# A mixer and mixture-of-experts layer on one core: 128-row score operands, another row order of the expert weights, fewer overflow branches, and the final norm in a branch of its own

## Chip, core and metric

The kernel runs as one program on 1 core of one Trainium2 chip. The metric is the device time of one execution in microseconds (us). Before the change three runs took 717.22, 716.81 and 714.42 us, median 716.81.

## What is computed

One layer over 256 tokens of 1024 channels, with 256 context tokens beside them, in float32. Cut to what matters here:

```
m = silu(c) @ w_mod + b_mod                       # six vectors: sh1 sc1 g1 sh2 sc2 g2
h = rms_norm(x) * (1 + sc1) + sh1                 # the same for the context tokens
gq, gk, gv, nq, nk, nv, fu, cu, gl = split(h @ w_in)
y_gqa = attention(8 query heads, 2 key/value heads, 256 + 256 keys)   # "g"
y_na  = neighbourhood attention, 8 heads                              # "n"
y_fn, y_cv = 2-D Fourier mixing, convolution of 31 taps
x = x + g1 * (sum of sigmoid(gate) * (branch @ w_branch)) @ w_out
h2 = rms_norm(x) * (1 + sc2) + sh2
# router: the best of 4 groups of experts, in it the best 2 of 4 experts
x = x + g2 * sum_e gate[:, e] * ((silu(a_e) * b_e) @ w_down[e]),  a_e, b_e = split(h2 @ w_gu[e])
out = rms_norm(x)                                 # the final norm
```

There are 16 experts; w_gu[e] is 1024x1024 and w_down[e] 512x1024, so each expert brings 6 MiB of weights, 96 MiB in all.

## The kernel before

**Up to the router.** SyncE (SP) streams weight tiles of 1 MiB. `product` (L290) multiplies them on TensorE in three passes, with a high and a low part of both operands made by ScalarE (L277) and VectorE (L278). Instructions are put in order ahead of time by a planner that sets the projection's matmuls between the steps of the attention, and on VectorE the taps of the convolution (L458) and the sums of the modulation (L194).

**Attention "g" (L482 to L505).** For 8 heads and 2 tiles of 128 queries each, so for 16 score tiles, the scores are two matmuls into one PSUM tile of 128x512. The first multiplies `qG`, which holds the high part of 64 channels in one half of its 128 rows and the low part in the other, by `kT`, the high part of the keys, stacked twice. The second adds high part by low part: it takes the 64 rows of `qG` with the high part and the 64 rows of `kTl`, the low part of the keys, of that group. Then come VectorE's maximum (L487), an exponential on ScalarE (L492), a reciprocal and a product on VectorE (L493, L494), four transposes (L497) and the product with the values (L505). `kTl` is written by one subtraction of 128x128 for each of four key tiles (`split`, L375), `kT` by copies of 64x128 (L385, L386).

**Experts.** They go in 8 pairs. `load_unit` (L630) brings 256 rows of a weight matrix as one tile [128 partitions, 2, 1024]; row k * 128 + p of the unit goes to partition p, so a partition gets two pieces of 4 KB. Up to 64 tokens of an expert are handled in fixed places, in two blocks of 32; the flags of the router say which pairs need the second block (`both`), which experts have more than 64 tokens (`fmore`, up to 128, summed by pair in `fpair`), and which more than 128 (`frest`). A pair's order of work is: the gather of the tokens for a group of 2 pairs (`group_step`, one-hot matmuls "gag" with 128 channels of `xh` and `xl` as the stationary operand), up products of block 1, `If(both)` block 2, `If` overflow up (`more_up`), scatter of the previous pair (adds on `xs`, L905), transposes of the hidden values (L815), **`If` overflow gather of the next pair** (`more_gather`), down products, `If(both)`, `If` overflow down (`more_down`). Each overflow `If` first asks for the pair (L1126) and within it for each expert (L1128). With the inputs here experts 5 and 13, in pairs 2 and 6, are the only ones with an overflow, and no expert has more than 128 tokens.

**End.** After the last scatter each engine with work in it meets `If(frest > 0)` (L1212), a long body that never runs here, and jumps over it. Then the final norm follows: four squares with sums on ScalarE (L1222), three short POOL instructions for each of two token tiles (L1225, L112, L113), four products on VectorE (L1229) and four output DMAs (L1230), two issued by ScalarE and two by SP.

Of the kernel before, what the change touches and what calls it, by code (L numbers as in the profile page):

```python
# [19 lines left out]
P = 128  # L20
D = 1024
# [29 lines left out]
PKW = _off  # L51


@with_exitstack
def mixer_moe(ctx: ExitStack, tc: tile.TileContext, A, out, dbg=None):
# [143 lines left out]
    def mod_cols(i, dst):  # L199

        res = []
        yield from mod_sums(i, res)
        t = pt("md", f"mt_{i}")
        for b in range(NK):
            PE.matmul(t[:, 2 * b : 2 * b + 2], res[0][:, P * b : P * (b + 1)], ones[:, 0:2], start=True, stop=True)
        V.tensor_tensor(dst, t[:, : 2 * NK].rearrange("p (b r) -> p b r", r=2)[:, :, 0],
                        pks("bm")[:, NK * i : NK * (i + 1)], op=ALU.add)
# [320 lines left out]
    def half(h, i):  # L528
# [5 lines left out]
              lambda h, t, i: qG[half(h // 4, i), h // 4, h % 4, 128 * t : 128 * t + 128],  # L534
              lambda h, i: (kTl[half(h // 4, 1)] if i else kT[:, h // 4]).rearrange("p k n -> p (k n)"),
# [156 lines left out]
    for c in range(4):  # L692
        accs = [mm_t(f"wo{c}{t}") for t in range(NT)]
        product(A["w_out"][:, 256 * c : 256 * c + 256], NK,
                [(accs[t][:, :256], tok_major((mh, ml), t)) for t in range(NT)], f"out{c}")
        cs = slice(256 * c, 256 * c + 256)
        for t in range(NT):
            xc = xs[:, t, cs]
            tmp = gp.tile([P, 512], F32, name=f"xo{c}{t}", tag="gt")
            V.tensor_tensor(tmp[:, :256], accs[t][:, :256], g1row[:, cs], op=ALU.mult)  # L700
            V.tensor_tensor(xc, xc, tmp[:, :256], op=ALU.add)
            tp = tr_t(f"x2tr{c}{t}")
            for k in range(2):
                PE.transpose(tp[:, 128 * k : 128 * (k + 1)], xs[:, t, P * (2 * c + k) : P * (2 * c + k + 1)], ident)
# [86 lines left out]
    def low_rows(k0, k1):  # L791
        s = slice(P * k0, P * k1)
# [7 lines left out]
    with tc.issue_after(last_route.ins if hasattr(last_route, "ins") else last_route):  # L800
        low_rows(0, 1)
# [49 lines left out]
    def gather_step(hg, oh, k, name):  # L851
# [108 lines left out]
    def more_gather(e):  # L960
# [20 lines left out]
        for k in range(NK):  # L981
            d = tp[:, CAP * k : CAP * (k + 1)]
            tr(d, rows[:CAP, k // 4, P * (k % 4) : P * (k % 4 + 1)], ident[:CAP, :CAP])
# [39 lines left out]
    def rest(e):  # L1023
# [26 lines left out]
        for f in range(4):  # L1050
            tr(tp[:, 128 * f : 128 * f + 128], si[:, 128 * f : 128 * f + 128], ident)
# [31 lines left out]
    def first_gather(k):  # L1083
        if k:
            with tc.issue_after(after_oh.ins if hasattr(after_oh, "ins") else after_oh):
                low_rows(k, k + 1)
# [37 lines left out]
    def more_of(pair, f):  # L1124

        with tc.If((fpair & (1 << (8 + pair))) > 0):  # L1126
            for e in (2 * pair, 2 * pair + 1):
                with tc.If((fmore & (1 << e)) > 0):  # L1128
                    f(e)
# [24 lines left out]
    for pair in range(NPAIR):  # L1154
# [9 lines left out]
        if pair == NPAIR - 2:  # L1164
            frest = nc.values_load(flags[0:1, 2:3], engines=engs + [ET.SP], min_val=0, max_val=top)
# [26 lines left out]
        if pair + 1 < NPAIR:  # L1192
            more_of(pair + 1, lambda e: rows_of.__setitem__(e, more_gather(e)))
# [10 lines left out]
        more_of(pair, lambda e: more_down(e, rows_of[e][1], si_of[e]))  # L1204
# [6 lines left out]

    with tc.If(frest > 0, label="rest"):  # L1212
# [3 lines left out]


    junk = ep.tile([P, 2, 512], F32, name="junk", tag="ys", bufs=1)
    fss = small.tile([P, NT, 2], F32, name="fss", tag="fss", bufs=1)
    for t in range(NT):  # L1220
        for h in range(2):
            SC.activation(junk[:, h, :], xs[:, t, 512 * h : 512 * h + 512], AF.Square,  # L1222
                          accum_out=fss[:, t, h : h + 1])
        fr = small.tile([P, 2], F32, name=f"fr{t}", tag="rs")
        G.tensor_tensor(fr[:, 0:1], fss[:, t, 0:1], fss[:, t, 1:2], op=ALU.add)  # L1225
        rstd_of(fr[:, 0:1], fr[:, 0:1], D, 1)
        for h in range(2):
            s = slice(512 * h, 512 * h + 512)
            V.scalar_tensor_tensor(xs[:, t, s], xs[:, t, s], fr[:, 0:1], fng[:, s], op0=ALU.mult, op1=ALU.mult)  # L1229
            (nc.sync if h else nc.scalar).dma_start(out[128 * t : 128 * t + 128, s], xs[:, t, s])  # L1230
# [33 lines left out]

def layout(i):
# [8 lines left out]
        n1g=_cols(f["norm1_g"][0]), n2g=_cols(f["norm2_g"][0]),  # L1274
# [5 lines left out]
        wr=f["w_router"].reshape(NK, P, NE).transpose(1, 0, 2).reshape(P, -1), rb8=rows(np.tile(f["router_bias"], NT)),  # L1280
        low4=rows(np.tile(np.tril(np.ones((4, 4)), -1).reshape(-1), 8)), mhalf=np.full((P, 2), -0.5),
        bm=_cols(f["b_mod"][0]),
# [41 lines left out]
```

## Time and profile before

| | |
|---|---|
| runs | 717.22, 716.81, 714.42 us |
| profiled execution, its own time | 722.76 us |
| span of the instructions in it | 721.0 us |
| TensorE busy | 640.1 us, 89% |
| VectorE, ScalarE, POOL busy | 412.8, 265.7, 71.9 us |

PE is TensorE's matmuls and PEld its weight loads, DVE is VectorE, ACT ScalarE, POOL GpSimd and SP SyncE; a "q" behind a name is that engine's sequencer, which handles branches. "Idle" in a row is the time in which the engine did nothing just before, and behind the arrow stands what ended it. The profiled execution is 5.95 us longer than the median of the runs.

### The profile page before, as it was taken

To read this page: it belongs to the slowest core of one execution; us is meant where nothing else is said; L and a number is where in the kernel's file an instruction comes from. 1 tells how busy PE (TensorE), PEld (TensorE's weight loads), DVE (VectorE), ACT (ScalarE), POOL (GpSimd) and SP (SyncE) were. 2 spreads that over 40 slices of the span, in tenths; PEclk is the share of its full clock that TensorE was granted. 3 is DMA by queue.
4 is the path that set the end of the run, shared out by engine and by line. 5 is a ranking of instruction groups with operands and counts; after the bars stand their busy time and mean duration, and the time that the engine had idled before them with its cause. 6 is when DMAs were issued, how large, how long until landed. Compare 5 with 4: busy or idle time off the path is not lost. (4 is left out here: it accounts for less than half of the span.)

```text
span 721.0 us, 12019 instructions
## 1 busy us (share of the span) xinstructions
PE 640.1 (89%) x4721; PEld 443.8 (62%) x4725; DVE 412.8 (57%) x806; ACT 265.7 (37%) x486; POOL 71.9 (10%) x112
## 2 busy tenths in 40 slices
PE   3769899999999998999999967889889979998992
PEld 0269899987887898989899952343324224333230
DVE  0179889988888787585766553351343243303334
ACT  2066947367755533343445441230012111300112
POOL 0123300021302000313111010000000000000001
PEclk9969999999999999999999988899989999999895
DMA  9794582533543696768698560999997999998001
GB/s 362 277 340 130 177 286 64 170 119 118 170 136 99 247 314 210 252 224 264 219 370 287 175 234 4 397 408 407 408 409 285 409 406 409 407 385 347 1 2 62
DMA packets 75121, 180.07 MB, mean 250 GB/s; under 512 B 3104, under 2 KB 39072, under 8 KB 74016
## 3 DMA queue, kind: packets, MB, share of 16 engines
q1 hardware_dynamic: 73232, 173.42, 66.0%
q0 software_dynamic: 1104, 3.15, 1.4%
q10 hardware_dynamic: 704, 2.42, 0.8%
q8 instruction: 52, 0.85, 0.5%
q14 instruction: 29, 0.24, 0.1%
HBM read 177.92 MB, written 1.05 MB: 248 GB/s over the span
## 5 line engine op out<-in xcount | busy, mean ns | idle before, releaser
L812 PE MATMUL gu<-we,hg 128*32 128x512 f32 x832 | 101.5, 606 | 3.7 <-PEq L1126 2.4
L290 PE MATMUL gl<-hhil,wl_gl 128*128 128x256 f32 x256 | 72.9, 287 | 1.8 <-DVE wl_gl L278 1.7
L290 PE MATMUL gl<-hhil,wh_gl 128*128 128x256 f32 x256 | 73.3, 287 | 0.0
L290 PE MATMUL gl<-hlol,wh_gl 128*128 128x256 f32 x256 | 72.3, 283 | 0.0
L812 PEld LDWEIGHTS gu<-we,hg 128*32 128x32 f32 x832 | 28.3, 111 | 68.5 <-issue 59.3
L812 PE MATMUL y<-we,hT 128*32 128x512 f32 x416 | 59.8, 649 | 6.1 <-PEq L1126 5.6
L277 ACT CAST wh_gl<-w_gl 128x1024 fp32r<-128x1024 f32 x32 | 33.1, 1049 | 50.0 <-PE gl L290 25.4
L458 DVE SCALAR_TENSOR_TENSOR cv<-zp,pk,cv 128x256 f32<-128x256 f32 x120 | 51.2, 478 | 0.2
L290 PEld LDWEIGHTS gl<-hhil,wl_gl 128*128 128x128 f32 x256 | 48.0, 188 | 3.9 <-DVE wl_gl L278 3.3
L290 PEld LDWEIGHTS gl<-hhil,wh_gl 128*128 128x128 f32 x256 | 48.1, 188 | 1.5 <-issue 1.5
L290 PEld LDWEIGHTS gl<-hlol,wh_gl 128*128 128x128 f32 x256 | 48.3, 189 | 0.5 <-issue 0.5
L290 PE MATMUL z<-y,wh_br 128*128 128x256 f32 x256 | 47.6, 283 | 0.0
L278 DVE TENSOR_TENSOR wl_gl<-w_gl,wh_gl 128x1024 fp32r<-128x1024 f32 x32 | 41.0, 1294 | 9.8 <-ACT wh_gl L277 9.6
L194 DVE SCALAR_TENSOR_TENSOR acc<-wv,csil,acc 128x512 f32<-128x512 f32 x56 | 40.3, 747 | 7.8 <-DMA wv<-in_w_mod_dram 7.8
L812 PEld LDWEIGHTS y<-we,hT 128*32 128x32 f32 x416 | 14.9, 115 | 42.2 <-issue 39.9
L290 PEld LDWEIGHTS z<-y,wh_br 128*128 128x128 f32 x256 | 39.6, 188 | 0.9 <-issue 0.7
L374 ACT CAST yh<-ys 64x512 fp32r<-64x512 f32 x32 | 19.7, 617 | 51.5 <-DVE ys L894 51.1
L290 PE MATMUL z<-y,wl_br 128*128 128x256 f32 x128 | 36.8, 289 | 1.5 <-DVE wl_br L278 1.5
L894 DVE SCALAR_TENSOR_TENSOR ys<-y,gsl,G 128x512 f32<-128x512 f32 x16 | 12.0, 750 | 37.5 <-PE y L812 17.3
L674 POOL TENSOR_TENSOR merged<-merged,gt 128x512 f32<-128x512 f32 x12 | 19.3, 1610 | 117.6 <-DVE gt L673 117.6
L876 DVE TENSOR_TENSOR si<-si,gu 128x256 f32<-128x256 f32 x16 | 6.6, 418 | 42.5 <-ACT si L875 42.5
L166 PE MATMUL mod<-wm,csil 128*32 128x512 f32 x64 | 15.2, 843 | 14.4 <-DVE csil L155 9.0
(411 smaller groups left out, 1514.0 us busy)
## 6 DMA issues: line engine op xcount, KB each, us to landing
we<-in_w_gu_dram SPq DMA_DIRECT2D x64, 1024.0 KB, 13.3
we<-in_w_down_dram SPq DMA_DIRECT2D x32, 1024.0 KB, 18.4
wv<-in_w_mod_dram SPq DMA_DIRECT2D x16, 1024.0 KB, 5.5
w_gl<-in_w_in_dram SPq DMA_DIRECT2D x16, 1024.0 KB, 5.7
wm<-in_w_mod_dram SPq DMA_DIRECT2D x8, 1024.0 KB, 9.4
w_br<-in_w_branch_dram SPq DMA_DIRECT2D x8, 1024.0 KB, 5.9
w_out<-in_w_out_dram SPq DMA_DIRECT2D x4, 1024.0 KB, 6.4
w_gq<-in_w_in_dram SPq DMA_DIRECT2D x2, 1024.0 KB, 8.1
```

What stands on the lines that cost most here:

```text
L166: PE.matmul(acc[32 * j : 32 * j + 32, :], csil[:, k, :], wm[:, 512 * j : 512 * (j + 1)], start=(k == 0), stop=(k == NK - 1))
L194: V.scalar_tensor_tensor(acc[:, s], wm[:, k % 2, s], csil[:, k, 0:1], acc[:, s], op0=ALU.mult, op1=ALU.add)
L277: SC.copy(w[0], raw[:, s])
L278: sub(w[1], raw[:, s], w[0].bitcast(F32), op=ALU.subtract)
L290: PE.matmul(dst, a, b, start=(k == 0 and wi + xi == 0), stop=(k == kt - 1 and wi == 1))
L374: SC.copy(hi, src)
L458: V.scalar_tensor_tensor(cv[:, ct, :], zp[:, ct, j : j + S], convw[:, ct, j : j + 1], cv[:, ct, :], op0=ALU.mult, op1=ALU.add)
L674: G.tensor_tensor(mt, mt, gts[c], op=ALU.add)
L812: tc.keep_in_program_order(PE.matmul(*a, **k))
L876: V.tensor_tensor(si, si, acc[:, n:], op=ALU.mult)
L894: V.scalar_tensor_tensor(ys, y, gsl, G2[flip], op0=ALU.mult, op1=ALU.mult)
```

## The change

Four things are changed. (1) `kTl` becomes as wide as `kT`: for each group 128 rows, zero in the half that the group doesn't use. The second score matmul then contracts over 128 rows. (2) A weight unit puts rows 2p and 2p + 1 into partition p, one piece of 8 KB. The channels that meet those rows are taken with stride 2 (`chan`) in everything that makes the other operand: gathers, transposes, the low part `xl`, and the packed constants. (3) The overflow gather of the next pair moves behind the down products and shares one outer `If` with the overflow down; the first pair's gather and up share one as well. (4) The final norm becomes a function. It stands in `If(fnone < 1)`, which TensorE doesn't take part in, straight behind the last scatter and ahead of the `rest` body; a second copy stands at the end of that body.

```diff
+def chan(k):
+    return slice(2 * P * (k // 2) + k % 2, 2 * P * (k // 2 + 1), 2)
...
-    kTl = kG[:, 1024:1536].rearrange("p (k n) -> p k n", k=4)
+    kTl = kG[:, 1024:2048].rearrange("p (g k n) -> p g k n", g=2, k=4)
+    for g in range(2):
+        hs = slice(64 - 64 * g, 128 - 64 * g)
+        SC.activation(kTl[hs, g], ident[hs].unsqueeze(1).to_broadcast([64, 4, P]), AF.Copy, scale=0.0)
...
-            split(kh, kTl[:, kt, :], tp[:, :P])
+            SC.copy(kh, tp[:, :P])
+            for g in range(2):
+                hs = slice(64 * g, 64 * g + 64)
+                V.tensor_sub(kTl[hs, g, kt], tp[hs, :P], kh[hs].bitcast(F32))
...
-              lambda h, t, i: qG[half(h // 4, i), h // 4, h % 4, 128 * t : 128 * t + 128],
-              lambda h, i: (kTl[half(h // 4, 1)] if i else kT[:, h // 4]).rearrange("p k n -> p (k n)"),
+              lambda h, t, i: qG[:, h // 4, h % 4, 128 * t : 128 * t + 128],
+              lambda h, i: (kTl if i else kT)[:, h // 4].rearrange("p k n -> p (k n)"),
...
-        nc.sync.dma_start(t, src.rearrange("(k p) n -> p k n", p=P))
+        nc.sync.dma_start(t, src.rearrange("(p k) n -> p k n", k=2))
...
-                mm(g, src[:, t, P * k : P * (k + 1)], oh[t], start=(i == 0), stop=(i == 2 * NT - 1))
+                mm(g, src[:, t, chan(k)], oh[t], start=(i == 0), stop=(i == 2 * NT - 1))
...
-            tr(tp[:, 128 * c : 128 * c + 128], si[:, 128 * c : 128 * c + 128], ident)
+            tr(tp[:, 128 * c : 128 * c + 128], si[:, c::2], ident)
...
+    def more_first():
+        with tc.If((fpair & (1 << 8)) > 0):
+            for e in of(0):
+                if_more(e, lambda e: (rows_for(e), up_for(e)))
...
+    def more_rest(pair):
+        two = pair + 1 < NPAIR
+        with tc.If((fpair & ((3 if two else 1) << (8 + pair))) > 0):
+            for e in of(pair):
+                if_more(e, lambda e: more_down(e, rows_of[e][1], si_of[e]))
+            if two:
+                for e in of(pair + 1):
+                    if_more(e, rows_for)
...
-            frest = nc.values_load(flags[0:1, 2:3], engines=engs + [ET.SP], min_val=0, max_val=top)
+            others = [ET.DVE, ET.Activation, ET.Pool, ET.SP]
+            frest = nc.values_load(flags[0:1, 2:3], engines=[ET.PE] + others, min_val=0, max_val=top)
+            fnone = nc.values_load(flags[0:1, 2:3], engines=others, min_val=0, max_val=top)
...
-        if pair == 0:
-            more_of(0, lambda e: rows_of.__setitem__(e, more_gather(e)))
-        more_of(pair, lambda e: si_of.__setitem__(e, more_up(e, rows_of[e][0])))
+        more_ups(pair) if pair else more_first()
...
-        if pair + 1 < NPAIR:
-            more_of(pair + 1, lambda e: rows_of.__setitem__(e, more_gather(e)))
...
-        more_of(pair, lambda e: more_down(e, rows_of[e][1], si_of[e]))
+        more_rest(pair)
...
+    def final_norm():
+        junk = ep.tile([P, 2, 512], F32, name="junk", tag="ys", bufs=1)
+        for t in range(NT):
+            ...
+    with tc.If(fnone < 1):
+        final_norm()
     with tc.If(frest > 0, label="rest"):
         for e in range(NE):
             with tc.If((frest & (1 << e)) > 0):
                 rest(e)
+        final_norm()
```

The transposes of the normalised rows (L704), the low part `xl` (L794, 16 instructions of 128x128 in both kernels) and the modulation's column matmuls (L205) take `chan` in the same way.

## Rows read from the trace of the kernel before

**Rows 1.** Stretches: length, then busy us by engine, granted clock, DMA share, GB/s.
```profile
60.00:90.00 30.00, 26.77 (x218) 25.69 (x216) 26.82 (x69) 25.16 (x62) 12.22 (x14) 1.00 0.49 149
148.00:185.00 37.00, 37.00 (x270) 27.75 (x270) 31.12 (x66) 26.60 (x54) 7.18 (x14) 1.00 0.31 99
260.00:275.00 15.00, 13.32 (x110) 13.02 (x109) 13.16 (x19) 6.20 (x8) 0.00 (x0) 1.00 0.71 239
450.00:690.00 240.00, 216.83 (x1508) 82.44 (x1512) 81.33 (x163) 39.98 (x77) 3.71 (x14) 0.95 0.89 352
```
**Rows 2.** Timeline of weight loads: start, us, engine, line, operands, shapes, idle before.
```profile
148.49 0.18 PEld L482 LDWEIGHTS sg<-kG,qG 64*128 64x128 f32 x1 [0.24 <-issue]
148.92 0.19 PEld L482 LDWEIGHTS sg<-kG,qG 128*128 128x128 f32 x1 [0.24 <-issue]
```
**Rows 3.** Waits of 148 to 185 us: total us, times, longest.
```profile
PEld sg L482 <- issue: 4.9, 21, 0.3
```
**Rows 4.** Timeline of TensorE, two scatter matmuls of 128 rows in a row.
```profile
468.35 0.39 PE L812 MATMUL sce<-yl,oTe 128*128 128x512 f32 x1
468.58 0.40 PE L812 MATMUL sce<-yh,oTe 128*128 128x512 f32 x1
```
**Rows 5.** Instructions of L385 and L375: ns min/median/max, first and last start.
```profile
L385 ACT CAST kG<-kh x8: 283/296/307, 81.8 to 92.2; 64x128 fp32r<-64x128 f32 x8
L385 ACT CAST qG<-qh x4: 610/616/621, 72.6 to 78.5; 64x512 fp32r<-64x512 f32 x4
...
L375 DVE TENSOR_TENSOR kG<-ktr,kh x4: 283/284/288, 81.6 to 91.8; 128x128 fp32r<-128x128 f32 x4
```
**Rows 6.** Timeline of TensorE, two steps of a gather.
```profile
472.37 0.28 PE L812 MATMUL gag<-ohg,xl 128*128 128x256 f32 x1
472.49 0.28 PE L812 MATMUL gag<-ohg,xh 128*128 128x256 f32 x1
```
**Rows 7.** Instructions of gather loads, and of L360 (stride 2) and L363 (contiguous).
```profile
L812 PEld LDWEIGHTS gag<-ohg,xh x64: 186/188/330, 429.9 to 613.1; 128*128 128x128 f32 x64
...
L360 DVE TENSOR_TENSOR ropet_q<-qq,rsq x4: 284/289/295, 56.0 to 73.9; 128x128 f32<-128x128 f32 x4
...
L363 DVE TENSOR_TENSOR kn<-kk,ropet_k x2: 286/286/287, 79.2 to 82.7; 128x128 f32<-128x128 f32 x2
```
**Rows 8.** Stretches with 8 KB pieces (first) and 4 KB pieces (second).
```profile
16.00:20.60 4.60, 2.00 (x3) 0.27 (x3) 1.24 (x2) 1.85 (x4) 2.58 (x6) 1.00 1.02 424
...
480.00:540.00 60.00, 54.33 (x360) 18.41 (x365) 19.48 (x37) 8.97 (x18) 0.53 (x2) 0.94 1.03 408
```
**Rows 9.** Idle time ahead of instructions that use expert weights: us, times.
```profile
  DMA we<-in_w_gu_dram: 1.9, 4
```
**Rows 10.** TensorE's waits of 440 to 721 us: total us, times, longest.
```profile
PE y L812 <- PEq L1126: 6.0, 9, 2.8
PE gs L812 <- PEq L1126: 3.3, 1, 3.3
...
PE gu L812 <- PEq L1126: 2.4, 5, 0.9
PE gav L812 <- DVE ohv L840: 1.7, 2, 0.9
```
**Rows 11.** ScalarE's sequencer at L1212: ns min/median/max, start us.
```profile
L1212 ACTq COMPARE_BRANCH  x1: 64/64/64, 703.1 to 703.1; - x1
L1212 ACTq EVENT_SEMAPHORE  x1: 17/17/17, 705.7 to 705.7; - x1
```
**Rows 12.** Timeline of all engines at the end.
```profile
708.68 0.69 DVE L905 TENSOR_TENSOR xs<-xs,sce 128x512 f32<-128x512 f32 x1 [0.17 <-PE sce L812]
711.67 0.63 ACT L1222 ACTIVATE junk<-xs 128x512 f32<-128x512 f32 x1 [7.34 <-DVEq L1212]
...
715.67 2.48 SPq L1230 DMA_DIRECT2D out_dram<-xs  x2
...
716.36 1.41 DVE L1229 SCALAR_TENSOR_TENSOR xs<-xs,fr,pk 128x512 f32<-128x512 f32 x2 [0.72 <-POOL fr L113]
```

More of the change, by code (lines that the diff above doesn't have):

```diff
@@ L204, in mod_cols @@
         for b in range(NK):
-            PE.matmul(t[:, 2 * b : 2 * b + 2], res[0][:, P * b : P * (b + 1)], ones[:, 0:2], start=True, stop=True)
+            PE.matmul(t[:, 2 * b : 2 * b + 2], res[0][:, chan(b)], ones[:, 0:2], start=True, stop=True)
         V.tensor_tensor(dst, t[:, : 2 * NK].rearrange("p (b r) -> p b r", r=2)[:, :, 0],
@@ L703, in mixer_moe @@
             for k in range(2):
-                PE.transpose(tp[:, 128 * k : 128 * (k + 1)], xs[:, t, P * (2 * c + k) : P * (2 * c + k + 1)], ident)
+                PE.transpose(tp[:, 128 * k : 128 * (k + 1)], xs[:, t, chan(2 * c + k)], ident)
             SC.copy(tmp[:, 256:], tp[:, :256])
@@ L790, in mixer_moe, with low_rows @@
             last_xh = SC.activation(xh[:, t, :], xs[:, t, :], AF.Copy, scale=rstd[:, t : t + 1])
-    def low_rows(k0, k1):
-        s = slice(P * k0, P * k1)
+    def low_rows(k):
+        s = chan(k)
         for t in range(NT):
@@ L800, in mixer_moe @@
     with tc.issue_after(last_route.ins if hasattr(last_route, "ins") else last_route):
-        low_rows(0, 1)
+        low_rows(0)
     dump("key", key)
@@ L982, in more_gather @@
             d = tp[:, CAP * k : CAP * (k + 1)]
-            tr(d, rows[:CAP, k // 4, P * (k % 4) : P * (k % 4 + 1)], ident[:CAP, :CAP])
+            tr(d, rows.rearrange("p h n -> p (h n)")[:CAP, chan(k)], ident[:CAP, :CAP])
         for k in range(NK):
@@ L1050, in rest @@
         for f in range(4):
-            tr(tp[:, 128 * f : 128 * f + 128], si[:, 128 * f : 128 * f + 128], ident)
+            tr(tp[:, 128 * f : 128 * f + 128], si[:, chan(f)], ident)
         hT = ep.tile([P, 512], F32, name=f"hTr{e}", tag="hT", bufs=1)
@@ L1085, in first_gather @@
             with tc.issue_after(after_oh.ins if hasattr(after_oh, "ins") else after_oh):
-                low_rows(k, k + 1)
+                low_rows(k)
         group_step(0, k)
@@ L1122, in mixer_moe, with if_more, of, rows_for @@
     rows_of, si_of = {}, {}
-    def more_of(pair, f):
-        with tc.If((fpair & (1 << (8 + pair))) > 0):
-            for e in (2 * pair, 2 * pair + 1):
-                with tc.If((fmore & (1 << e)) > 0):
-                    f(e)
+    def if_more(bit, f):
+        with tc.If((fmore & (1 << bit)) > 0):
+            f(bit)
+    def of(pair):
+        return (2 * pair, 2 * pair + 1)
+    def rows_for(e):
+        rows_of[e] = more_gather(e)
+    def up_for(e):
+        si_of[e] = more_up(e, rows_of[e][0])
+    def more_first():
+        with tc.If((fpair & (1 << 8)) > 0):
+            for e in of(0):
+                if_more(e, lambda e: (rows_for(e), up_for(e)))
+    def more_ups(pair):
+        with tc.If((fpair & (1 << (8 + pair))) > 0):
+            for e in of(pair):
+                if_more(e, up_for)
+    def more_rest(pair):
+        two = pair + 1 < NPAIR
+        with tc.If((fpair & ((3 if two else 1) << (8 + pair))) > 0):
+            for e in of(pair):
+                if_more(e, lambda e: more_down(e, rows_of[e][1], si_of[e]))
+            if two:
+                for e in of(pair + 1):
+                    if_more(e, rows_for)
     def scatter_pair(pair):
@@ L1210, in mixer_moe @@
     scatter_pair(NPAIR - 1)
+    fss = small.tile([P, NT, 4], F32, name="fss", tag="fss", bufs=1)
+    def final_norm():
+        junk = ep.tile([P, 2, 512], F32, name="junk", tag="ys", bufs=1)
+        for t in range(NT):
+            for h in range(2):
+                SC.activation(junk[:, h, :], xs[:, t, 512 * h : 512 * h + 512], AF.Square,
+                              accum_out=fss[:, t, h : h + 1])
+            fr = fss[:, t, 2:3]
+            G.tensor_tensor(fr, fss[:, t, 0:1], fss[:, t, 1:2], op=ALU.add)
+            rstd_of(fr, fr, D, 1)
+            for h in range(2):
+                s = slice(512 * h, 512 * h + 512)
+                V.scalar_tensor_tensor(xs[:, t, s], xs[:, t, s], fr, fng[:, s], op0=ALU.mult, op1=ALU.mult)
+                (nc.sync if h else nc.scalar).dma_start(out[128 * t : 128 * t + 128, s], xs[:, t, s])
+    with tc.If(fnone < 1):
+        final_norm()
     with tc.If(frest > 0, label="rest"):
@@ L1215, in mixer_moe @@
                 rest(e)
[L1218 to L1230, printed above, removed]
+        final_norm()
 def _rope_tables():
@@ L1262, in _cols, with _pairs @@
     return np.asarray(v).reshape(-1, P).T
+def _pairs(v):
+    v = np.asarray(v).reshape(-1, P, 2, *np.asarray(v).shape[1:])
+    return np.moveaxis(v, 1, 0).reshape(P, -1)
 def layout(i):
@@ L1279, in layout @@
         qg=rows(qg), qgs=rows(swap(qg)), kg=rows(kg), kgs=rows(swap(kg)),
-        wr=f["w_router"].reshape(NK, P, NE).transpose(1, 0, 2).reshape(P, -1), rb8=rows(np.tile(f["router_bias"], NT)),
+        wr=_pairs(f["w_router"]), rb8=rows(np.tile(f["router_bias"], NT)),
         low4=rows(np.tile(np.tril(np.ones((4, 4)), -1).reshape(-1), 8)), mhalf=np.full((P, 2), -0.5),
-        bm=_cols(f["b_mod"][0]),
+        bm=np.concatenate([(_pairs if s in (3, 4) else _cols)(f["b_mod"][0][D * s : D * (s + 1)]) for s in range(6)], axis=1),
         slot=np.stack([32 * (np.arange(P) // 64) + np.arange(P) % 32 + 1, 32 * (1 - np.arange(P) // 64) + np.arange(P) % 32 + 1,
```

2 lines of the change are left out of this document (1 added, 1 removed).

## Prediction

> **What bounds the kernel now.** I read the page's busy times first, then the busy times by stretch, then the waits and timelines of the stretches that the diff touches, and last the end. TensorE is the bound almost everywhere. In the attention it is busy all 37.00 of 37.00 us, and VectorE is second with 31.12 [rows 1]; from 450 to 690 us it is busy 216.83 of 240 us, with the DMA engines at 0.89 of their share [rows 1]. Its idle time among the experts is mostly put down to its own sequencer at L1126, the question whether a pair has an overflow, and hardly to weights that come late: 1.9 us in four waits [rows 9, 10]. After the last scatter TensorE counts no more; there a chain of ScalarE, POOL, VectorE and two DMAs ends the span [rows 12]. So the edits are worth what they take off TensorE before 708 us, and off that chain after it.
>
> **Score matmuls.** The first and second score matmul alternate between 128 and 64 rows, and the weight load of each starts only when the matmul before it has begun its last part: two loads lie 0.43 us apart (148.49 and 148.92), each with 0.24 us of idle ahead of it [rows 2]. Two matmuls of the same 128x512 with 128 rows on both sides lie 0.23 us apart, 468.35 to 468.58, with nothing idle between them [rows 4]. If 128 rows everywhere bring that step, each of the 32 matmuls (8 heads, 2 query tiles, 2 passes) gives back 0.43 - 0.23 = 0.20 us, 6.4 us in all. Counted by the idle loads alone it is less: 21 of them with 4.9 us [rows 3], at 0.20 us each 4.2 us; the rest of the stall falls on loads of other products that come behind a 64-row matmul. TensorE is without a gap here, so this is on the path. But what is late next is VectorE: its 31.12 us would stand in 37 - 6.4 = 30.6 us, so it can't follow at once; some of its work can run behind, because it is fuller here than later, until 260 to 275 us, where TensorE already loses 1.68 of 15 us and VectorE has 13.16 [rows 1]. I take -5, between 0 (VectorE takes it all back) and -6.4.
>
> **Making the wide low keys.** ScalarE gets two fills of 64x512, like the casts at 0.62 us [rows 5]: 1.2 us, at any time before 82 us. VectorE gets eight subtractions of 64x128 for four of 128x128 at 0.284 [rows 5]; both have 128 elements in a partition, so I expect no shorter ones, and four more at 0.28 are 1.1 us. Both stand in a stretch where TensorE has 3.2 of 30 us idle, and VectorE and ScalarE have 3.2 and 4.8 [rows 1]; TensorE's product goes on with work that doesn't need the keys. I take +0.5, between 0 (hidden) and +2.3 (all of it on the path).
>
> **Stride 2.** Four group gathers of 8 x 4 matmuls are 128 loads from `xh` and `xl` with stride 2. Today such a load takes 0.188 us and the step from one matmul to the next is 0.12 [rows 6, 7], so the loads overlap and set the pace together with the matmul. No load with a stride stands in the trace. The nearest row is VectorE's: 128x128 from a source with stride 2 takes 0.289 us and the same size without it 0.286 [rows 7]. By that row the cost is 0, and I take 0; the other end is a load that takes twice as long, 128 x 0.12 = +15.4 us. Transposes and the low part `xl` have few instructions and the same answer. Below nothing there is no gain: nothing gets shorter. [...]
>
> **One piece of 8 KB.** The stretch with 8 KB pieces moved 424 GB/s and the one with 4 KB 408 [rows 8]: 4% of a stream that TensorE waits for during 1.9 us in four waits [rows 9]. I take -0.3, between 0 and -1.9.
>
> **Branches.** Before there are 24 overflow `If`s: first gather, 7 gathers, 8 ups, 8 downs; 6 are entered (gather, up and down of two experts). TensorE's waits for L1126 sum to 3.3 + 6.0 + 2.4 = 11.7 us [rows 10], so a skipped one costs 11.7 / 18 = 0.65 us on the mean, unevenly: the longest are 3.3 and 2.8. After there are 16. Of the 8 that go, 6 are skipped today: 6 x 0.65 = 3.9 us. Against that, the four merged branches that are entered (pairs 1, 2, 5, 6) now ask for two more experts; I put that at 0.4 each, an estimate below the mean of an outer skip, 1.6 us. The two gathers themselves stay on the path at their new place; their wait for VectorE's one-hot, 1.7 us in two [rows 10], may go, since the down products now run meanwhile, and the overflow up comes a whole first block of products later, so the gather isn't late there. I count half of that, since VectorE must also pass the branch: -0.8. Sum -3.9 + 1.6 - 0.8 = -3.1. Because single skips cost from nothing to 3.3 us and every instruction now stands elsewhere in the program, I take half, -1.5, between -6 and +6.
>
> **The end.** The last add on `xs` ends at 708.68 + 0.69 = 709.37, yet the first square starts only at 711.67, 7.34 us after ScalarE's last work [rows 12], because VectorE must jump over the `rest` body before the norm can see it. The four squares follow one another, so the last starts about 711.67 + 3 x 0.63 = 713.56. With the norm ahead of the body the first three run beside the scatter and the last starts at 709.4: 4.15 us sooner, and POOL, VectorE and DMA follow as they do now. The jump doesn't go away, it comes behind the norm. ScalarE's takes 703.1 to 705.7, 2.6 us [rows 11]; SP has to make its jump after the last output DMA is issued. The DMA takes 2.48 us to land [rows 12]. If jump and landing overlap, nearly all of the 4.15 is kept; if the jump comes behind the landing, 4.15 - 2.6 = 1.5 is. I take -2, between 0 and -4.15. The extra register loads stand on engines that have idle time; POOL gets a branch in the shadow of the same jump.
>
> **Sum.** -5 + 0.5 + 0 - 0.3 - 1.5 - 2 = -8.3 us on the profiled execution: 722.76 - 8.3 = 714.5. That execution is 5.95 us above the median of the runs shown, so the forecast for the time is 716.81 - 8.3 = 708.5, with 704.5 to 712.5 as its own range.
>
> **Rivals.** (B) VectorE bounds the attention and takes the gain back: 716.81 - 8.3 + 5 x 0.8 = 712.5, up to 713.5 if all of it. For it: 31.12 against 30.6. Against it: TensorE doesn't wait for VectorE in that stretch at all now, so there is some lead.
>
> (C) Strided loads cost twice: 708.5 + 15.4 = 724, slower than before. Its place is the 128 gather matmuls, its price 0.12 us each, and from 8.3 / 128 = 0.065 us each on the change no longer gains. For it: the loads already take longer than the step, so any lengthening shows. Against it: VectorE's equal rows.
>
> (D) Skips turn into long ones. A merged body is longer, so a skip jumps further, and TensorE's skips show two kinds, under 0.9 us and about 3 [rows 10]. If the four skipped merged branches (pairs 0, 3, 4, 7) each cost 2.8 in place of 0.65, that is +8.6: 708.5 + 8.6 = 717, no change. Against it: the body stays a small part of what is jumped at L1212. [...]
>
> (E) All goes well: attention -6.4, end -4.1, branches -5: 701.5.
>
> (F) The change doesn't do what it says: the step of 0.43 comes from something other than the row count, such as both passes summing into one tile. For it: loads of 128 rows wait as long as those of 64 [rows 2]. Against it: the scatter's matmuls are such a sum too, at 0.23. Then 713.5.
>
> **Chances.** Forecast 0.53, B 0.12, C 0.09, D 0.10, E 0.10, F 0.06. Half a per cent, 3.6 us, is about what can be told from no change; faster means below 713.2, slower above 720.4. Nearly all of the forecast, E, most of B, half of F and a little of D are faster: 0.74. Slower is C and a trace of D: 0.10. The rest is 0.16. The range 701 to 717 leaves out C, the upper half of D and the lower end of E.
>
> **What would show it.** Right: 32 score matmuls at steps of 0.23, no idle ahead of their loads, the attention's stretch 5 to 6 us shorter, gather steps still 0.12, the last square just behind the last add, and fewer L1126 waits. Wrong: waits of TensorE for L487, L493 or L494 in the attention (B), gather steps of 0.2 or more (C), waits of 2 to 3 us for the sequencer behind several pairs (D), or an end as long after the last add as the 11.6 us of now.

## The result: 0.9% slower, and the profile after

Eleven runs of the changed kernel have a median of 723.43 us (718.46 to 725.01), eleven of the kernel before 715.47 us (714.42 to 719.35); the ratio is 1.009 with a 95% interval of 1.0069 to 1.011. The forecast was 708.5 us, range 701 to 717. The two profiled executions hide this: 722.56 us after, a usual one, and 722.76 before, which lies 7 us over the median of its own kernel. So the traces are compared by stretches, and what a stretch is worth is tested with further kernels.

Lengths in us, each from the first start of one product to the first start of another, or to the last end, read from the instruction listings of the profiles. cb and nk are products of the input projection, sg and sn the score products of the attentions "g" and "n". "1+2+4" is the changed kernel with the branches of before (experiment e5), "last" is the version of experiment e16.

| stretch | before | changed | 1+2+4 | last |
|---|---|---|---|---|
| first cb to first nk product (the keys of "g" are made) | 27.9 | 31.9 | 31.8 | 28.8 |
| first sg to first sn product (attention "g") | 53.6 | 49.2 | 49.5 | 49.1 |
| first sn product to first gather product | 228.2 | 226.1 | 225.4 | 225.1 |
| first gather product to end of TensorE's work (experts) | 278.7 | 285.2 | 278.8 | 276.1 |
| end of TensorE's work to end of span | 12.3 | 9.9 | 10.0 | 10.2 |

The scores and the final norm do what they say, and two places take it back: the stretch where the keys are made, and the experts. Each column is one execution. The experts, with the branch code of before, took from 272.9 to 279.0 us in the profiles of the kernel before and of e1, e2, e4 and e7, so a difference of a few us there says little by itself.

The stretches of the changed kernel, with columns as in [rows 1]:

```profile
60.00:90.00 30.00, 25.43 (x182) 23.68 (x182) 25.84 (x68) 22.84 (x57) 12.09 (x14) 0.89 0.51 166
148.00:185.00 37.00, 36.08 (x307) 32.34 (x306) 33.89 (x73) 28.57 (x57) 8.46 (x15) 1.00 0.48 158
450.00:690.00 240.00, 214.22 (x1486) 81.48 (x1485) 79.36 (x158) 39.07 (x75) 3.20 (x12) 0.96 0.84 344
```

From 148 to 185 us 307 matmuls are done where it were 270, and VectorE is at 33.89 of 37. From 60 to 90 us it is the other way: 182 for 218, and the granted clock, 1.00 before, is 0.89. The weight loads of the scores, where [rows 2] showed 0.24 us of idle ahead of each:

```profile
150.12 0.77 PEld L494 LDWEIGHTS sg<-kG,qG 128*128 128x128 f32 x4
150.94 0.19 PEld L295 LDWEIGHTS nq<-hhil,wh_nq 128*128 128x128 f32 x1
```

Four loads in 0.77 us and no idle between them; the four matmuls, the first at 150.24, take 1.09 us, a step of 0.23. Now TensorE's timeline in the stretch of the keys, the rows with idle time ahead of them:

```profile
79.00 0.39 PE L295 MATMUL cb<-hhil,wl_cb 128*128 128x256 f32 x1 [0.19 <-DVE wl_cb L283]
81.05 0.30 PE L442 MATMUL ktr<-pk,kn 128*128 128x128 f32 x1 [0.60 <-DVE kn L368]
82.39 0.58 PE L295 MATMUL cb<-hhil,wh_cb 128*128 128x256 f32 x1 [1.05 <-ACT wh_cb L282]
83.49 0.47 PE L442 MATMUL ktr<-pk,kn 128*128 128x128 f32 x1 [0.30 <-DVE kn L440]
84.62 0.58 PE L295 MATMUL cb<-hhil,wl_cb 128*128 128x256 f32 x1 [0.66 <-DVE wl_cb L283]
```

Five short waits in 6 us, three of them for the cast and the low part of a weight, and matmuls of 0.58 us: at a granted clock of 1.00 (77.8 to 80.4 us) those of cb take 0.27 to 0.39, and from 83 to 88 us, at 0.50, they take 0.41 to 0.58. The order on ScalarE, first in the kernel before, then in the changed one:

```profile
79.09 1.05 ACT L277 CAST wh_cb<-w_cb 128x1024 fp32r<-128x1024 f32 x1
81.33 0.26 ACT L374 CAST kh<-ktr 128x128 fp32r<-128x128 f32 x1
```
```profile
78.59 0.25 ACT L444 CAST kh<-ktr 128x128 fp32r<-128x128 f32 x1
81.28 1.06 ACT L282 CAST wh_cb<-w_cb 128x1024 fp32r<-128x1024 f32 x1
```

The last cast of `w_cb` stood ahead of the first key tile and now stands behind it. The instructions of the new low keys and of the gather, columns as in [rows 5, 7]:

```profile
L447 DVE TENSOR_TENSOR kG<-ktr,kh x8: 278/288/295, 79.1 to 92.0; 64x128 fp32r<-64x128 f32 x8
...
L422 ACT ACTIVATE kG<-pk x2: 624/627/630, 71.8 to 73.7; 64x512 fp32r<-64x512 f32 x2
```
```profile
L824 PEld LDWEIGHTS gag<-ohg,xh x64: 192/198/331, 425.6 to 614.4; 128*128 128x128 f32 x64
```

The durations are those that the prediction used. A load with stride 2 takes 198 ns against 188 [rows 7]; 128 of them are 1.3 us at most, and the steps of the last three group gathers grew from 0.121 or 0.122 to 0.124 us, on the mean of 31 steps. TensorE's waits among the experts (440 us to the end before, 420 us to the end here):

```profile
PE gav L824 <- DVE ohv L852: 4.5, 2, 2.7
...
PE gu L824 <- issue: 3.4, 1, 3.4
PE gs L824 <- PEq L1151: 2.9, 1, 2.9
PE gu L824 <- PEq L1156: 2.8, 5, 1.4
...
PE y L824 <- PEq L1137: 2.0, 2, 1.0
...
PE y L824 <- PEq L1163: 1.3, 3, 0.9
```

What was L1126 with 11.7 us [rows 10] is now L1151, L1156, L1137 and L1163 with 9.0 (L1137 also has the questions for single experts, L1128 before); but the one-hot of the overflow gather stands at 4.5 where it was 1.7, and 3.4 us have no cause in the profile ("issue"). The places of both, in TensorE's timeline (20 of the 32 down products of pair 1 stand ahead of the moved gather, the other 12 behind it):

```profile
471.59 2.77 PE L824 MATMUL y<-we,hT 128*32 128x512 f32 x20 [0.16 <-issue]
477.03 0.41 PE L824 MATMUL gav<-xh,ohv 128*64 128x512 f32 x1 [2.67 <-DVE ohv L852]
...
588.42 1.94 PE L824 MATMUL gu<-we,hg 128*32 128x512 f32 x8 [3.44 <-issue]
```

And the stretches around them, first of the changed kernel, then of the same work in 1+2+4:

```profile
471.40:486.00 14.60, 11.76 (x66) 4.32 (x69) 4.26 (x12) 3.67 (x8) 0.00 (x0) 0.77 1.02 420
588.00:607.00 19.00, 18.40 (x132) 6.14 (x132) 0.97 (x4) 0.77 (x2) 0.00 (x0) 0.84 1.01 420
```
```profile
467.00:482.00 15.00, 12.99 (x98) 7.41 (x102) 6.73 (x16) 6.17 (x12) 0.00 (x0) 1.00 1.02 421
584.00:600.00 16.00, 15.81 (x135) 4.93 (x134) 4.13 (x7) 2.01 (x4) 0.00 (x0) 1.00 1.01 418
```

The clock column is the reading that counts: behind a stop of 2.67 or 3.44 us TensorE works on at a mean of 0.77 and 0.84 of the full clock. Behind the first, the work of 478 to 484.5 us ran at a granted clock of 0.51; in e11, the same kernel with its code shifted, the same work behind a stop of 2.52 us ran at 1.00:

```profile
478.00:484.50 6.50, 6.50 (x33) 2.68 (x31) 2.31 (x7) 1.95 (x5) 0.00 (x0) 0.51 1.02 423
```
```profile
478.80:485.00 6.20, 6.20 (x45) 3.13 (x49) 1.94 (x6) 1.79 (x4) 0.00 (x0) 1.00 1.01 419
```

From the gate product (`gs`) of pair 1 to the first up product of pair 2 the changed kernel takes 22.4 us, e11 19.6 and 1+2+4 19.1. So against 1+2+4 the moved gather cost 3.3 us there in one and 0.5 in the other. From the gate product of pair 4 to that of pair 5 the changed kernel takes 31.6 us and 1+2+4 29.0, which has a stop of its own there, ahead of the last down products of pair 4, and a lower clock behind it:

```profile
580.72 3.30 PE L824 MATMUL y<-we,hT 128*32 128x512 f32 x12 [2.61 <-PEq L1138]
```

The two stretches are 5.9 of the 6.4 us by which the experts of these two traces differ.

The end answers to [rows 12]:

```profile
710.84 0.69 DVE L917 TENSOR_TENSOR xs<-xs,sce 128x512 f32<-128x512 f32 x1 [0.17 <-PE sce L824]
...
711.62 0.63 ACT L1256 ACTIVATE junk<-xs 128x512 f32<-128x512 f32 x1
...
712.96 2.76 SPq L1264 DMA_DIRECT2D out_dram<-xs  x2
...
713.94 1.41 DVE L1263 SCALAR_TENSOR_TENSOR xs<-xs,fss,pk 128x512 f32<-128x512 f32 x2 [1.00 <-POOL fss L118]
```

The last square starts 0.09 us behind the last add (711.53), and the span ends 9.2 us behind it where it was 11.6. The last product of the norm ends 3.8 us behind that add where it was 8.4 [rows 12]; from there to the end of the span it is 5.4 us where it was 3.2.

### The profile page after: what moved, and what is told of

Read it like the earlier page. It is cut to its first block, busy times and chain, and to the rows that moved or that the text cites. A ratio compares the mean times of both kernels' runs of the same rounds, so it can differ in the third digit from the quotient of the medians.

```text
span 720.7 us, 12056 instructions
## 1 busy us (share of the span) xinstructions
PE 638.2 (89%) x4720; PEld 447.7 (62%) x4725; DVE 415.7 (58%) x810; ACT 267.0 (37%) x488; POOL 72.0 (10%) x112
## 5 line engine op out<-in xcount | busy, mean ns | idle before, releaser
L824 PEld LDWEIGHTS gu<-we,hg 128*32 128x32 f32 x832 | 28.8, 112 | 73.5 <-issue 66.7
L887 ACT ACTIVATE si<-gu 128x256 f32<-128x256 f32 x16 | 6.0, 383 | 64.0 <-PE gu L824 52.8
```

Of the source, the lines that this page charges most:

```text
L824: tc.keep_in_program_order(PE.matmul(*a, **k))
L887: SC.activation(si, acc[:, :n], AF.Silu)
```

## The experiments

A ratio is that of the kernel's runs to runs of the kernel before on the same chip, with its 95% interval; all were timed in five rounds. The reasons were tested in four steps. The letters of rivals and theories in these expectations are their own, not those of the prediction.

### Which part costs it

Each part of the change alone, put into the kernel before with the lines of the diff above: e1 the score matmuls and `kTl`, e2 the units with `chan`, e3 the merged branches, e4 the final norm.

> The kernel before with the wide low keys alone (part 1). Theory 1 (the merged overflow branches cost the time: with them VectorE is late at the one-hot of the moved gather, 4.5 us in two waits where it was 1.7, and the down products of block 2 wait 1.0 us twice behind the merged body) expects this part to keep what the two traces show in the attention, 3 to 6 us less than before. Rival 2 (no part costs anything by itself; it is where the code and the clock happen to fall) expects 0 to -6 too. Rival 3 (the weight units with their stride cost it) expects the same. If this part is the slow one, it shows 2 us or more above the kernel before.

> The kernel before with the expert units of neighbouring rows and their stride-2 operands alone (part 2). Theory 1 expects -1 to +1 us: gather steps went from 0.118 to 0.120 us only. Rival 2 expects within 3 us either way. Rival 3 expects +4 to +8 us, with the loss among the experts.

> The kernel before with the merged overflow branches alone (part 3). Theory 1 expects +5 to +10 us over the kernel before, among the experts, with the waits for the one-hot of the moved gather at 4 us or more and the wait of 1.0 us behind each merged body that is entered. Rival 2 expects within 3 us. Rival 3 expects -1 to +1 us.

> The kernel before with the final norm in its own branch alone (part 4). All theories expect -1.5 to -3 us, since the time from the end of the last add on the residual to the end of the span is 11.6 us before and 9.2 us after. Half a us or less, or slower, would say that the moved norm costs something ahead of the end, in the loads of the flags or in the branches.

Measured: scores 0.9969 (0.9939 to 0.9999), units 0.9996 (0.9967 to 1.0025), branches 1.0058 (1.003 to 1.0087), norm 0.9979 (0.9949 to 1.0008). Only the branches cost, 4.2 us, which lies between what rival 2 and theory 1 expected, with the wait for the one-hot at 4.3 us in two as theory 1 said; the intervals of the units and the norm include no change. The scores gave 2.2 us, less than theory 1 expected and within what rival 2 did. The parts sum to about nothing, and together they took 6 to 8 us. In e1 the attention is 49.5 us for 53.6, and the stretch of the keys 31.2 for 27.9: the gain is paid back there.

The other way round, e5 is the changed kernel with the branches of before:

```diff
-        more_rest(pair)
+        more_of(pair, lambda e: more_down(e, rows_of[e][1], si_of[e]))
```

(and the gathers and ups at their old places), and e6 the kernel before with the gather moved and nothing merged:

```diff
-        if pair + 1 < NPAIR:
-            more_of(pair + 1, lambda e: rows_of.__setitem__(e, more_gather(e)))
...
         more_of(pair, lambda e: more_down(e, rows_of[e][1], si_of[e]))
+        if pair + 1 < NPAIR:
+            more_of(pair + 1, lambda e: rows_of.__setitem__(e, more_gather(e)))
```

> The changed kernel with the merged overflow branches taken out again (parts 1, 2 and 4). Alone the merging took 4.2 us, but the four parts alone sum to +0.2 us where all together took +8.0, so 8 us belong to no part. Theory 1 (the merging is what costs, and costs more in the longer program) expects -3 to -5 us against the kernel before, the sum of the other three (-2.2, -0.3, -1.5). Rival 2 (the 8 us come from where code and clock happen to fall, whichever part it is) expects about 0 to +4. Rival 4 (the wide low keys and the moved norm disturb each other) expects +2 or more.

> The kernel before with the overflow gather of the next pair put behind the overflow down, in an If of its own, and nothing merged: 24 overflow branches as before. Theory 1a (the place costs: behind the down products TensorE has nothing left to do while it passes its branches and waits for the one-hot, and its clock falls) expects +3 to +6 us, with the wait for the one-hot at 4 us or more in two. Theory 1b (the merging costs: the inner questions and longer jumps) expects 0 to +1.

e5: 0.9998 (0.9977 to 1.002). e6: 1.0081 (1.0047 to 1.0115). So without part 3 the loss is gone, all of it, and moving the gather alone costs as much as moving and merging. That e5 is no faster than before was a miss of theory 1: the other three parts gain nothing together in these runs. Rival 2, the place of code and clock, expected just that.

The time of e6 speaks against theory 1b and is what 1a expected, but its trace isn't. Where 1a expected 4 us or more at the one-hot, it has

```profile
PE gav L812 <- DVE ohv L840: 1.3, 2, 0.7
```

and the granted clock around the gather (475.8 to 490 us) is 1.00. From the gate product of pair 1 to that of pair 2 e6 takes 41.7 us, before it was 41.5, the changed kernel takes 44.9 and e3 44.4. So by these traces the long stop ahead of the moved gather comes with moving and merging together, and not with moving alone. Its experts are 4.7 us longer than before, about 1 us in each of several pairs. Part of that is seen in the 12 down products that stand behind the questions in pairs 2 and 3, first before, then in e6:

```profile
530.27 3.63 PE L812 MATMUL y<-we,hT 128*32 128x512 f32 x12
...
564.94 1.91 PE L812 MATMUL y<-we,hT 128*32 128x512 f32 x12 [0.19 <-PEq L1126]
```
```profile
529.98 5.34 PE L812 MATMUL y<-we,hT 128*32 128x512 f32 x12
...
565.66 3.04 PE L812 MATMUL y<-we,hT 128*32 128x512 f32 x12 [0.19 <-PEq L1126]
```

What costs the rest in e6 stays open; it ran at one placing of its code.

### Is it the one-hot?

The profile names VectorE's one-hot as what TensorE waited for. e9 gives it a second buffer:

```diff
-        oh = onehot(f"v{e}", lambda t: key[:, t, e : e + 1], CAP, "ohv", 1)
+        oh = onehot(f"v{e}", lambda t: key[:, t, e : e + 1], CAP, "ohv", 2)
```

(two small tiles were joined to make room), and e10 asks for the gathers first:

```diff
-            for e in of(pair):
-                if_more(e, lambda e: more_down(e, rows_of[e][1], si_of[e]))
             if two:
                 for e in of(pair + 1):
                     if_more(e, rows_for)
+            for e in of(pair):
+                if_more(e, lambda e: more_down(e, rows_of[e][1], si_of[e]))
```

> The changed kernel with two buffers for the one-hot of the overflow gather in place of one, so that VectorE can write it without waiting for TensorE to pass the expert before. The profile puts 4.5 us of TensorE's waits down to that one-hot (two waits, the longer 2.7). Theory A (the late one-hot is the cost) expects -3 to -5 us against the changed kernel, near +4 against the kernel before. Theory B (TensorE passes five branches one after another with nothing queued, 0.5 us each, and the one-hot is only what it meets last) expects no more than 0.7 us less than the changed kernel, so +7 to +8 against the kernel before, with TensorE's idle time ahead of the moved gather still over 2 us.

> The changed kernel with the two questions of the merged body in the other order: first the gather of the next pair, then the overflow down. Theory B expects the idle time ahead of the moved gather to fall by the two inner questions that then come later, about 1 us in each of pairs 1 and 5, and by as much again if the granted clock then stays up in pair 1 (it was 0.77 over 14.6 us there): -1 to -5 us against the changed kernel, +3 to +7 against the kernel before. Theory A expects the same as the changed kernel, since the one-hot is no earlier relative to TensorE.

e9: 1.0054 (1.0029 to 1.0079), and its profiled span, 720.7 us, is the changed kernel's to the tenth. VectorE's timeline and TensorE's waits in it:

```profile
472.30 0.36 DVE L852 SCALAR_TENSOR_TENSOR ohv<-pk,key 128x64 fp32r<-128x64 f32 x2 [1.07 <-DVEq L1138]
```
```profile
PE gav L824 <- PEq L1138: 4.5, 2, 2.7
```

The one-hot is written at 472.3, 4 us sooner, and TensorE waits the same 4.5 us, now put down to its own sequencer. The time alone, 3.9 us over the kernel before, is what theory A expected (near +4) and not B (+7 to +8). But the wait that A wanted to shorten is as long as ever, so A falls by the trace; the 2.6 us to the changed kernel's ratio it doesn't explain, and they are less than the placing moves below. In the changed kernel the one-hot waited for TensorE, as its own view (what it sat idle for: us, times) says:

```profile
  PEq L1137: 12.5, 2
```

It shared a buffer with the expert before, whose skipped branch TensorE had yet to pass. In the changed kernel's trace TensorE's sequencer asks its five questions (the pair, two experts' downs, two experts' gathers) from 474.6 to 476.9 us, some 0.5 us each, and the 20 down products ahead of them end at 474.4. With the gathers first, e10 is at 0.9979 (0.9953 to 1.0005), 1.1% under the changed kernel; the wait for the gather is 1.9 us in two and the clock in that stretch 0.89:

```profile
469.50:482.00 12.50, 9.98 (x61) 3.85 (x65) 3.53 (x11) 2.94 (x7) 0.00 (x0) 0.89 1.02 421
```

That is 8 us, more than theory B expected (-1 to -5 us). Also gone in e10 was the 3.4 us stop ahead of pair 5: 4.9 of the 7.1 us by which its experts are shorter lie between the gate products of pairs 4 and 5. Neither of the two has an overflow, so their merged body isn't entered and its order can't matter; that the other layout of TensorE's code is the reason is tested next.

### Is it where the code stands?

e11, e12 and e15 put 64, 128 and 32 small matmuls ahead of all of TensorE's work, at 8.8 us, not long before the changed kernel's waits for weights of 1.03 us (to 11.88) and 1.97 us (to 15.78); each is two instructions (e11's profile counts 12184 instructions where the changed kernel's counts 12056), so later code stands 128, 256 and 64 instructions further on. e13 and e14 do the same with 64 for the kernel before and for 1+2+4.

```diff
+    zt = sc_t("shift")
+    for _ in range(64):
+        PE.matmul(zt[:, 0:2], ident16, ident16[:, 0:2], start=True, stop=True)
```

> The changed kernel with 64 small matmuls (128 instructions of TensorE) ahead of its first one, in the first 10 us, where TensorE waits for weights; all later code of TensorE stands 128 instructions later. In the changed kernel TensorE stands still for 3.4 us at 585 us, with nothing to wait for in the profile, where the kernel before stood still for 2.8 us at 583.7 behind a branch. Theory C (these stops are the loading of instructions, and their place hangs on where the code falls) expects the stop to be at another place or gone and the time 0 to 5 us off the changed kernel's. Rival D (the stop belongs to that place in the work) expects it at the same product, and the time within 1 us.

> The changed kernel with 128 small matmuls at its start, so all of TensorE's later code stands 256 instructions later. [...]

> The kernel before with the 64 small matmuls (128 instructions). If the changed kernel's loss is the placing of code, then the kernel before has its own draw: theory C expects the long stops behind its branches at 446.3 (3.3 us) and 583.7 (2.8 us) to move or vanish, and a time from 6 us less to 6 us more. Rival D expects it unchanged within 1.5 us.

> Parts 1, 2 and 4 without the merged branches, with the 128 instructions ahead. Together with the shifted changed kernel (-0.24%) it tells the price of the merging at a second placing. Theory A' (the merging costs by itself, 3 us or more) expects it at -0.7% or lower against the kernel before. Theory C (the merging costs little, the placing costs) expects -0.6 to +0.6%, with no order between it and the shifted changed kernel.

> The changed kernel with 32 small matmuls (64 instructions) at its start: a third placing. Theory C expects a time between the two that are known, -0.5% to +1% against the kernel before, with the long stops in places of their own. Rival D expects +0.9%, as the changed kernel.

| shift in instructions | before | 1+2+4 | changed |
|---|---|---|---|
| 0 | 1 | 0.9998 (0.9977 to 1.002) | 1.009 (1.0069 to 1.011) |
| 64 | | | 1.0026 (1.0005 to 1.0048) |
| 128 | 0.9995 (0.9971 to 1.0018) | 1.0000 (0.9978 to 1.0023) | 0.9976 (0.995 to 1.0002) |
| 256 | | | 1.0047 (1.0025 to 1.0069) |

The first up product of pair 5 in e12 (256) and e11 (128), then the long stop that e11 has in pair 0, and the one of e15 (64), at the last down products of pair 4:

```profile
587.43 2.78 PE L827 MATMUL gu<-we,hg 128*32 128x512 f32 x24 [3.40 <-issue]
```
```profile
583.51 1.92 PE L827 MATMUL gu<-we,hg 128*32 128x512 f32 x16
...
450.44 1.93 PE L827 MATMUL y<-we,hT 128*32 128x512 f32 x8 [4.62 <-PEq L1166]
```
```profile
585.39 2.42 PE L827 MATMUL y<-we,hT 128*32 128x512 f32 x12 [3.89 <-PEq L1166]
```

And the same place of pair 0 in e13 and e14:

```profile
452.67 1.93 PE L815 MATMUL y<-we,hT 128*32 128x512 f32 x8 [6.84 <-PEq L1129]
```
```profile
453.14 1.88 PE L827 MATMUL y<-we,hT 128*32 128x512 f32 x5 [5.86 <-PEq L1141]
```

With 128 instructions more the stop leaves pairs 4 and 5, and one of 4.6 to 6.8 us stands in pair 0, in all three kernels; with 64 it is a little earlier in the work, with 256 it is back where it was, to the product. So the long stops of TensorE's sequencer go by where its code stands: a shift of 128 or 64 moves them, and one of 256 brings the 3.4 us stop back. That is theory C as to the place, and rival D falls; that a stop is the loading of instructions, as theory C has it, no run here shows. The time followed less closely than the place. e11 moved it by 8 us, where theory C had 0 to 5; at 256 it is half of the loss, +0.47%, since behind the returned stop pair 5's products took 15.1 us and not 17.9. e14 speaks against theory A' (-0.7% or lower).

The stop ahead of the moved gather does not go by the placing: it is 2.67, 2.59, 2.52 and 2.68 us in the four. What does is the other stops and the clock. The experts of the changed kernel and of e11:

```profile
425.60:710.80 285.20, 251.06 (x1691) 97.36 (x1696) 99.86 (x215) 47.63 (x94) 4.73 (x18) 0.94 0.73 298
```
```profile
424.90:702.70 277.80, 244.45 (x1691) 95.20 (x1696) 99.84 (x215) 47.61 (x93) 4.61 (x18) 0.96 0.75 305
```

TensorE is idle for 34.1 and 33.4 us, nearly the same; its busy time differs by 6.6, and a granted clock of 0.94 and 0.96 leaves about 17 and 11 us of these stretches unused, an estimate from the two rows. So in this pair of traces the 7.4 us are nearly all clock: the stops add up alike, but the clock falls behind fewer of them.

Over four placings the changed kernel is at -0.24, +0.26, +0.47 and +0.9%, 1+2+4 at two at 0.0. The mean of the four is +0.35%, 2.5 us. That is an estimate of moving and merging by itself, and a loose one: the four values spread over 8 us, more than any part of the change is worth. It also means that e1 to e4 can't be read as the price of a part to better than a few us, e3's +4.2 and e6's +5.8 included.

### Where the attention's gain went

In e1 and in the changed kernel the two zero fills (1.25 us on ScalarE) stand among the weights' casts, and in the planner's order the last cast of `w_cb` comes behind the first keys. e7 is part 1 alone with the fills on POOL, e8 the same with parts 2 and 4, e16 as e8 with `kG` and its fills set up ahead of the queries' loop.

```diff
-        SC.activation(kTl[hs, g], ident[hs].unsqueeze(1).to_broadcast([64, 4, P]), AF.Copy, scale=0.0)
+        G.tensor_scalar_mul(kTl[hs, g], ident[hs].unsqueeze(1).to_broadcast([64, 4, P]), 0.0)
```

> Part 1 alone, as in the first experiment, but the two zero fills of the wide low keys written by POOL in place of ScalarE. In the first experiment the stretch from the first cb product to the first nk product took 31.2 us where the kernel before has 27.9, with the fourth cast of that weight behind the first keys on ScalarE. Theory 5 (the fills push the casts of the weights behind the keys, and that costs what the attention gains) expects the stretch back at 28 us and -4 to -6 us against the kernel before. Rival 6 (the eight subtractions on VectorE cost it) expects the stretch at 30 us or more and -1 to -3 us.

> Parts 1, 2 and 4 with the fills on POOL and the branches as before: the version that the experiments point to. Theories 1 and 5 together expect -5 to -9 us against the kernel before (attention -4.3, norm -2.3, units 0 to -1). If code and clock rule (rival 2), it is within 3 us of the kernel before.

> As the version with fills on POOL and no merged branches (parts 1, 2 and 4), with the two fills written earlier, before the queries are normalised. In the last version with fills on POOL they took 3.1 us there right ahead of the keys' norms, and TensorE waited 2.8 us behind that. Theory 5 expects the stretch from the first cb to the first nk product at 28 us, the attention at 49.6 us, the end at 10 us, and -4 to -7 us against the kernel before. If VectorE takes the attention's gain back later (the stretch from the first z to the first wo product was 159 us in the kernel before and 160 to 161 us with the fills on POOL), it is -1 to -4 us.

e7: 1.0017 (0.9984 to 1.0051), a miss, and the stretch at 30.8 us is what rival 6 expected. The casts are back in their order, but on POOL the fills take 3.1 us right ahead of the keys' norms. VectorE waits for these, with the queries' rotation behind them, and TensorE for that; POOL's, VectorE's and TensorE's rows of e7:

```profile
71.29 3.07 POOL L417 TENSOR_SCALAR kG<-pk 64x512 fp32r<-64x512 f32 x2
```
```profile
75.48 0.25 DVE L431 TENSOR_SCALAR kk<-kk,kr 128x64 f32<-128x64 f32 x1 [2.70 <-POOL kr L113]
```
```profile
76.13 0.66 PE L406 MATMUL qtr<-pk,qr 128*128 128x128 f32 x4 [2.81 <-DVE qr L363]
```

e8: 0.9978 (0.9952 to 1.0004), 1.6 us where theories 1 and 5 expected 5 to 9 and rival 2 no more than 3, with the stretch of the keys at 30.8 us as in e7. In e16 the fills start at 39.8 and 43.9 us, behind two of POOL's low parts of a weight and well ahead of the norms:

```profile
L399 POOL TENSOR_SCALAR kG<-pk x2: 1553/1737/1921, 39.8 to 43.9; 64x512 fp32r<-64x512 f32 x2
```

The stretch of the keys is 28.8 us, the attention 49.1, and the time 711.29 us, ratio 0.9922 (0.9896 to 0.9947): 5.6 us less than before, faster than the kernel before and than the changed one at any of its four placings. Theory 5 is borne out for the stretch, and rival 6 falls, since the eight subtractions are still there: two fills in the wrong place had taken 3.0 of the 4.4 us that 32 matmuls gave back. The ratios of e5 and e16 differ by 5.4 us, though; what gave the rest isn't shown. The experts, with the same branch code, are 2.7 us shorter in e16's trace than in e5's, and it was tried at one placing only.

## Why the prediction was wrong, step by step

**The step that failed is the branches**, forecast at -1.5 between -6 and +6. By the ratios of the changed kernel and e5 it is 1.009 / 0.9998, +0.92% or 6.6 us, just beyond its upper bound. The count was right, and the sequencer's waits did fall, from 11.7 to 9.0 us. Wrong was, first, the sentence that the gather's wait for the one-hot "may go, since the down products now run meanwhile". In the changed kernel the one-hot itself waited for TensorE's sequencer (e9): ahead of the down products the passage had cost two waits of 0.9 us at most [rows 10]; behind them, with the questions of the merged body in a row, it is one stop of 2.67 us in pair 1 and one of 1.8 in pair 5. Wrong was, second, that idle time was priced at its length: behind the stop in pair 1 the clock fell to 0.51 (478 to 484.5 us), and the stretch grew by 3.3 us where the stop is 1.8 us longer than the wait it replaced. Third, the placing was in the range as "every instruction now stands elsewhere", but as noise around half the sum; it moved the time by 8 us, and by the mean of the four placings (2.5 us, an estimate) it is the larger part of the 6.6. What e6 lost by the move alone is not explained.

**Making the keys**, +0.5 between 0 and +2.3, measured +3.9. Its durations were right and the reason was not: the stretch had 3 us of idle time on every engine [rows 1], and I took that as cover. The planner's order put the fills ahead of a cast that TensorE needed. This step is beyond its upper bound too.

**Scores**: -5 forecast, -4.4 measured in the stretch (53.6 to 49.2), with VectorE near full as said. The mechanism was right and the rivals B and F fall: 128 rows bring the step of 0.23, VectorE takes nothing back there, and the stretch behind it, to the first gather product, is no longer than before (226.1 us for 228.2).

**Stride 2**: 0 forecast; 10 ns a load, about 0.3 us in the gathers' steps. Rival C is out, though its 724 us came nearest to the time measured: that is luck, for its reason is refuted. **Units**: -0.3; the wait for weights went from 1.9 us [rows 9] to 1.7, and e2 shows no gain that can be told from nothing. **End**: -2 forecast, -2.4 measured in the traces, -1.5 in e4 with an interval that includes no change. The squares start 4.1 us sooner, as reckoned, and 2.2 us are lost again behind the norm's last product, where the jump over `rest` now stands; that the jump is what takes them is argued, not shown.

One account stays open. By the stretches the scores, the keys and the end add up to -2.9 us, but 1+2+4 took as long as the kernel before at both placings, with intervals of 0.2%. Some 3 us are lost in it elsewhere.

**Rival D** of the prediction (717 us) named the sequencer and had a chance of 0.10. It came nearer than the forecast, but it expected longer skips of the four merged bodies that are not entered. What happened is a stop at the entered ones of pairs 1 and 5, and others at places that the layout sets, in the kernel before as well.

## What to carry to other kernels

A wait's releaser can itself be waiting for the engine that waits: before pricing a move by it, look at what the releaser sat idle for (here VectorE's one-hot for TensorE's sequencer, 12.5 us in two). A stop of TensorE of 2 to 3 us is to be priced with the clock that may fall behind it: here the same stop cost 0.5 us in one placing, with the clock at 1.00 behind it, and 3.3 in another, with 0.51. And where a kernel has branches, a difference of 1% between two versions may be the place of the code (here a shift alone gave 1.1%): shift the code without changing the work before a part gets the credit or the blame.

## What the runs showed that I had not expected

The place of TensorE's code moved one kernel by 1.1% (1.009 to 0.9976) with nothing else changed. A stop of 6.84 us behind a single branch stood in a run whose time was the same as before (e13, 0.9995), while other stops had shortened or gone (3.27 to 1.57 us ahead of pair 0's gate product, 2.77 us in pair 4). After a stop of 3.4 us the next 19 us ran at 0.84 of the full clock in one kernel, while in another (e12) the same stop at the same product left the work behind it (587 to 603 us) at 1.00. The stop ahead of pair 2's gather did the same in the changed kernel (0.51 behind it) and e11 (1.00). What decides it stays open.
